# Places of moving operands modulo 256 bytes, and the order of two column widths, in a TensorE-bound decoder layer

## The chip, the core and the metric

The kernel runs on one core of one Trainium2 chip, in one launch. The metric is the device time of that launch in microseconds; the median of the runs shown is compared. The work is spread over the core's engines as the profile names them: PE (TensorE matmuls) with PEld (its weight loads), DVE (VectorE), ACT (ScalarE), POOL (GpSimd), and SP (SyncE, which here issues the DMAs).

## The reference

One layer of a decoder is computed for 1,024 prompt tokens and 64 sample tokens that share all weights:

```python
h = rmsnorm(x, norm_mix)
q, k, v, gu, gv, ga, gb = split_in(h @ w_in)
o = windowed attention of q, k, v          # window 128, per-head sinks
s = spatial_gating(gelu(gu), layernorm(gelu(gv)), ws, bs)
merged = sigmoid(ga) * (o @ w_pa) + sigmoid(gb) * (s @ w_pb)
x = x + merged @ w_out
z = rmsnorm(x, norm_ffn) @ w_up            # 5632 columns
c = conv_b + sum(zp[:, j:j + T] * conv_w[j] for j in range(3))
a, b = split(c)
x = x + (gelu(a) * b) @ w_down
y = rmsnorm(x, norm_final)
```

The model is 1,024 wide and the inner width of the feed-forward part is 2,816. Keys, values, the convolution's tails and the normalised gating values are further outputs.

## The kernel before

All data is float32. Every large product is made of three TensorE passes on split operands: an operand is split into a high part (written by ACT as type float32r) and a low part (the rest, by DVE), and high·high, high·low and low·high are added up in PSUM. The helper `split` at line 39 makes both parts; the names end in `h` and `l`. In each pass a 128×128 weight tile is loaded (LDWEIGHTS, one for every matmul) and a moving tile of 256, 288, 320 or 512 columns streams through.

The 1,088 tokens are worked in two groups: group 0 has 576 tokens (the 64 samples and 512 prompt tokens), group 1 has 512. The large projections use one level of a Strassen-like scheme of seven products on half-sized blocks. Its moving operands, called T, are sums of token blocks: for each of four inner blocks `kk` there are seven planes, of 288 columns for group 0 and of 256 columns for group 1, each in a high and a low version. The work runs through these stages:

1. The gating and value columns for all tokens (line 519, moving tiles of 256 columns).
2. The other columns of `w_in` by the seven products (`Chain.product`, matmul at line 301). A chain is one product's 12 matmuls: four `kk` times the three passes, all on one PSUM bank. For most weight pairs the chain of group 0 (12 matmuls of 288 columns) is followed by that of group 1 (12 of 256) on the same weights: 13 pairs × 7 products in this stage. For three weight pairs each group goes alone.
3. The gating branch and attention (lines 1168 to 1219), with the branch projection `branch` between, then two projections in `merge` and the output projection. Their matmuls stand in `mm3` at line 238: chunks of 320 and 256 columns for group 0, of 512 columns for group 1. The attention's product with the values at line 1219 has moving tiles of 512 columns as well.
4. The up projection, again `Chain.product` at line 301: 19 weight pairs with both chains, and three for which each group goes alone.
5. The down projection, also by seven products (`mm_dn`, matmul at line 1671). For each inner block `x` and each of four output blocks `m`, three matmuls of 288 columns (`e` = 0) stand before three of 256 (`e` = 1), from one T tile of 544 columns. The last four inner blocks of the last product are worked one width after the other.

So line 301 runs 32 × 7 = 224 products with a chain of 288 and a chain of 256 columns behind it, 42 chains of 288 columns alone and 42 of 256 alone.

What the change touches is where tiles lie in SBUF. A tile pool hands out addresses one after the other; `line(pool, n)` at line 246 takes n bytes of each partition that nobody uses, so that what is allocated next starts n bytes further. A weight tile starts in both programs at byte 32 modulo 256 (the addresses here and below are those that the two built programs carry). A T plane of group 0 has 288 × 4 = 1,152 bytes, which is 128 modulo 256; one of group 1 has 1,024 bytes, 0 modulo 256. In the kernel before the high T planes of one `kk` are one tile of seven planes and the low ones another, so that from plane to plane a group-0 operand lies 128 bytes further, modulo 256. Those are `t0_job` (line 653) for stage 2 and `t0_split` (line 1418) for stage 4.

Of the kernel before, what the change touches and what calls it, by code (L numbers as in the profile page):

```python
# [7 lines left out]
F32R = mybir.dt.float32r  # L8
# [7 lines left out]
P = 128  # L16
# [18 lines left out]
def layer(tc, a):  # L35
# [13 lines left out]
    with ExitStack() as top:  # L49
# [204 lines left out]

        def right(stack, name, bufs=1):
            return stack.enter_context(tc.tile_pool(name=name, bufs=bufs, side="right", reuse_waits="tile"))

        def combine(t4, b11, b12, b21, b22, eng=G):

# [107 lines left out]
        with ExitStack() as ph1:  # L367
# [285 lines left out]
            def t0_job(kk):  # L653
                def go():
                    first, t4, rest = sums_of(0, kk)
                    txa[0][kk] = th, tl = tuple(t0h.tile([P, 7, 288], F32R, name=f"t{y}{kk}") for y in "hl")
                    split(th[:, 0], tl[:, 0], first)
                    split(th[:, 1:5], tl[:, 1:5], t4)
                    split(th[:, 5:7], tl[:, 5:7], rest)
                    if kk == 3:  # L660
                        line(t0h, 32)
                return go

            def t1_job(kk):
# [322 lines left out]
            kvp["p"] = kvo.enter_context(tc.tile_pool(name="kv", bufs=1, reuse_waits="tile"))  # L987
            prep = prepare(groups[0])
            m1 = mo[1].enter_context(tc.tile_pool(name="mlp1", bufs=1, reuse_waits="tile"))
            line(m1, 64)  # L990
            b_order = [(0, 0), (1, 0), (0, 1), (1, 1)] + [(c, g) for c in range(2, KD) for g in range(2)]
            sgs, bst = {}, {}

# [55 lines left out]
            def attention(gr, pieces):  # L1049
# [102 lines left out]
                with tc.tile_pool(name=f"at{g}", bufs=1) as ap:  # L1152
                    steps = [(kv, i) for kv in range(NKV) for i in range(nblk)]
                    st = {}

                    def sc_p(kv, i):
                        if i == 0 and not has_s:
                            oh[kv], ol[kv] = (act.tile([P, 2, n], F32R, name=f"o{x}{kv}") for x in "hl")
                        b = gr["blk0"] + i
                        cur = P * i + (P if g else 0)  # L1160
                        k0 = cur - P if b else cur
                        o0 = 0 if b else P
                        ps = psm.tile([P, 1024], F32, name="sc")
                        ps = ps.rearrange("p (h j) -> p h j", h=4)
                        for h in range(4):
                            q = qt[2 * kv + h // 2][:, h % 2, P * i:P * i + P]
                            for e in range(2):
                                PE.matmul(ps[:, h, o0:256], q, kst[kv][:, e, k0:cur + P],  # L1168
                                          start=e == 0, stop=e == 1)
                        if i == 0 and kv:  # L1170
                            operands(gr, kv + 1)()
                        s = ap.tile([P, 4, P + 1], F32, name="s", bufs=3)
                        G.tensor_copy(s[:, :, P], late["sinkb"][:, 4 * kv:4 * kv + 4])
                        S.copy(s[:, :, 0:P], ps[:, :, P:256])
                        if b:
                            V.copy_predicated(s[:, :, 0:P], late["mprev"].to_broadcast([P, 4, P]),
                                              ps[:, :, 0:P])
                        else:
                            G.affine_select(s[:, :, 0:P], s[:, :, 0:P], [[0, 4], [-1, P]], ALU.is_ge, NEG,
                                            base=0, channel_multiplier=1)  # L1180
                        nm = ap.tile([P, 4], F32, name="nm", bufs=3)
                        V.tensor_reduce(nm, s, AX.X, ALU.max, negate=True)
                        dn = ap.tile([P, 4], F32, name="dn", bufs=3)
                        for h in range(4):
                            S.activation(s[:, h], s[:, h], AF.Exp, bias=nm[:, h:h + 1],  # L1185
                                         accum_out=dn[:, h:h + 1])
                        V.reciprocal(dn, dn)
                        V.tensor_mul(s[:, :, 0:P], s[:, :, 0:P], dn[:, :, None].to_broadcast([P, 4, P]))
                        st[kv, i] = s

                    def tr_p(kv, i):
                        s = st.pop((kv, i))
                        pt = psp.tile([P, 512], F32, name="pt")
                        for h in range(4):
                            PE.transpose(pt[:, h * P:h * P + P], s[:, h, 0:P], ident)  # L1195
                        ph = ap.tile([P, 512], F32R, name="ph")
                        pl = ap.tile([P, 512], F32R, name="pl")
                        split(ph, pl, pt)
                        b = gr["blk0"] + i
                        prev = vst[b - 1 if b else 0]  # L1200
                        parts = [(prev, ph), (prev, pl)]
                        if b:
                            for src, nm in ((ph, "h"), (pl, "l")):
                                t = ap.tile([P, 512], F32R, name=f"c{nm}")
                                G.affine_select(t.rearrange("p (h q) -> p h q", h=4),
                                                src.bitcast(F32).rearrange("p (h q) -> p h q", h=4),
                                                [[0, 4], [1, P]], ALU.is_ge, 0.0, base=0,
                                                channel_multiplier=-1)
                                parts.append((dvst[b], t))
                        st[kv, i] = parts  # L1210

                    def pv_p(kv, i, last):
                        if not last:
                            po = psp.tile([P, 512], F32, name="po")
                            st[kv, i] = po, st[kv, i]
                        po, parts = st[kv, i]
                        for e in (len(parts) - 1,) if last else range(len(parts) - 1):
                            v, t = parts[e]
                            PE.matmul(po, v[:, kv, :], t, start=e == 0, stop=last)  # L1219
                        if not last:  # L1220
                            return
                        st.pop((kv, i))
                        t = ap.tile([64, 512], F32, name="ot")
                        S.copy(t, po[64:128])
                        of = ap.tile([P, 2, P], F32, name="of", bufs=2)
                        tv = t.rearrange("p (a r q) -> p a r q", a=2, r=2)
                        pv = po[0:64].rearrange("p (a r q) -> p a r q", a=2, r=2)
                        for par in range(2):
                            V.tensor_add(of[64 * par:64 * par + 64], pv[:, :, par], tv[:, :, par])
                        c0 = soff + P * i  # L1230
                        split(oh[kv][:, :, c0:c0 + P], ol[kv][:, :, c0:c0 + P], of)

                    for i in range(len(steps) + 2):
                        if i >= 2:
                            tr_p(*steps[i - 2])
                        if i >= 3:
                            pv_p(*steps[i - 3], True)
                        fill()
                        if i < len(steps):
                            sc_p(*steps[i])  # L1240
                        fill()
                        if i >= 2:
                            pv_p(*steps[i - 2], False)
                    pv_p(*steps[-1], True)
# [26 lines left out]
            hmo = [ExitStack(), ExitStack()]  # L1271
            hmp = [hmo[g].enter_context(tc.tile_pool(name=f"hm{g}", bufs=1, reuse_waits="tile")) for g in (1, 0)][::-1]
            for pool in hmp:
                line(pool, 128)
            ms = [[], []]

            def operand(g):
# [140 lines left out]
            def t0_split(kk):  # L1418

                def go():  # L1420
                    x0, x1, t4 = hx.pop(kk)
                    tx[0][kk] = th, tl = tuple(t0p.tile([P, 7, 288], F32R, name=f"t{y}0{kk}") for y in "hl")
                    if kk % 2:
                        line(t0p, 96)
                    split(th[:, 0], tl[:, 0], x0[:, 0:288])
                    split(th[:, 5:7], tl[:, 5:7], x1.rearrange("p (h c) -> p h c", h=2))
                    split(th[:, 1:5], tl[:, 1:5], t4)
# [221 lines left out]
        with ExitStack() as ph3:  # L1649
# [9 lines left out]
                    nc.sync.dma_start(x[:, m], x1d[4 * dh + m][:, HT * th:HT * th + HT])  # L1659

            spans = ((0, 288), (288, HT))

            def place(m, e):
                b = bank[m] if e == 0 else bank[4 + m // 2]
# [109 lines left out]
            for at, j in enumerate(DN_ORDER):  # L1774
# [4 lines left out]
                for lo, hi in blocks:  # L1779
# [14 lines left out]
                    for mp in range(2) if hi - lo == 2 else (0,):  # L1794
                        for x in range(lo, hi):
                            for m in range(2 * mp, 2 * mp + 2) if hi - lo == 2 else range(4):
                                for e in range(2):
                                    mm_dn(m, e, x, got[x - lo], new)
                        if hi == NU:
                            for m in (2 * mp, 2 * mp + 1):  # L1800
# [109 lines left out]
```

## Time and profile before

| | before |
|---|---|
| runs, us | 1522.74, 1518.06, 1524.00 |
| median, us | 1522.74 |
| profiled execution: first to last instruction, us | 1519.4 |
| PE busy, us (share, matmuls) | 1503.9 (99%, 11,528) |
| PEld busy, us (share) | 1461.9 (96%) |
| DVE busy, us (share) | 1175.9 (77%) |
| ACT busy, us (share) | 850.5 (56%) |
| POOL busy, us (share) | 266.6 (18%) |

The profiled execution's own time is its span, 1519.4 us from the first to the last instruction; that is 3.3 us under the median of the runs and inside their spread. Times in the trace count from the span's start. An entry of a group of instructions names the line, the engine, the operation, the tiles (out, then in), the shapes and the count, then the busy time in us and the mean length of one in ns. The lengths of matmuls overlap, since they are pipelined: 0.28 to 0.30 us is shown for one that is followed by the next after 0.11 to 0.14 us. What a matmul costs is therefore read from the start of one row to the start of another, divided by the number of matmuls between them.

### The profile page before, as it was taken

Reading aid. Unit: us, or ns where it says so; the run is one execution under the profiler, and the core shown is the slowest. Engines: PE = TensorE matmul, PEld = TensorE weight load, DVE = VectorE, ACT = ScalarE, POOL = GpSimd, SP = SyncE. Lnnn points to the kernel's source line nnn. Section 1 sums busy time; section 2 is a strip of 40 time slices with the busy share of each in tenths; the row PEclk is TensorE's granted clock in tenths of the full one; section 3 lists DMA queues with packets and bytes.
Section 4 is the critical chain, followed back from the end, with each engine's and each line's share of the span. In section 5 each row is a group of like instructions: output and inputs, shape, how many; then the busy total and the mean of one; then the engine's idle time right before and its main releaser. Section 6 shows DMA issues by size and latency. Waiting matters only on the chain.

```text
span 1519.4 us, 30105 instructions
## 1 busy us (share of the span) xinstructions
PE 1503.9 (99%) x11528; PEld 1461.9 (96%) x11528; DVE 1175.9 (77%) x1897; ACT 850.5 (56%) x1767; POOL 266.6 (18%) x382
## 2 busy tenths in 40 slices
PE   9999999999999999999999999999999999999997
PEld 9999999999998989988989999999999999999997
DVE  7798877655576877979568988898898888785686
ACT  7557676654465675764344555655555556453452
POOL 0001000010030222210134322332132222000002
PEclk9999999999999999999999999999999999999999
DMA  7687446864779757449988333332232216973463
GB/s 253 210 280 272 154 164 222 243 212 142 245 245 290 223 162 250 153 138 308 330 281 278 129 117 116 124 116 100 108 128 104 108 58 234 367 251 97 117 182 122
DMA packets 135232, 289.88 MB, mean 191 GB/s; under 512 B 15537, under 2 KB 36849, under 8 KB 135089
## 3 DMA queue, kind: packets, MB, share of 16 engines
q1 hardware_dynamic: 134944, 287.96, 57.0%
q8 instruction: 90, 1.47, 0.4%
q14 instruction: 54, 0.43, 0.1%
q10 hardware_dynamic: 144, 0.01, 0.0%
HBM read 198.97 MB, written 90.92 MB: 191 GB/s over the span
## 4 chain that ended last, share of the span: by engine, by line
PE 84%; DVE 4%; DMA 4%; ACT 3%; issue 3%; POOL 1%; SPq 0%; POOLq 0%; ACTq 0%; DVEq 0%
PE st L301 44%; PE mm L238 15%; PE dn L1671 13%; PE st L519 6%; PE po L1219 2%; PE sc L1168 1%; DVE wl L41 1%; DMA v<-gvd 1%; PE pt L1195 1%; DMA wl<-upd 1%; POOL x L1734 1%; PE mx L803 1%; DMA vnd<-v 1%; ACT wh L41 1%; ACT s L1185 1%
## 5 line engine op out<-in xcount | busy, mean ns | idle before, releaser
L301 PE MATMUL st<-th,wh 128*128 128x288 f32 (+1 forms) x2128 | 611.6, 287 | 3.1 <-ACT kn L282 2.1
L301 PE MATMUL st<-tl,wh 128*128 128x288 f32 (+1 forms) x2128 | 609.4, 286 | 0.0
L301 PE MATMUL st<-th,wl 128*128 128x288 f32 (+1 forms) x2128 | 609.1, 286 | 0.3 <-DMA wl<-upd 0.3
L301 PEld LDWEIGHTS st<-th,wh 128*128 128x128 f32 x2128 | 400.3, 188 | 5.1 <-ACT kn L282 2.5
L301 PEld LDWEIGHTS st<-th,wl 128*128 128x128 f32 x2128 | 399.9, 188 | 0.5 <-DMA wl<-upd 0.5
L301 PEld LDWEIGHTS st<-tl,wh 128*128 128x128 f32 x2128 | 400.0, 188 | 0.0
L1671 PE MATMUL dn<-th,wh 128*128 128x288 f32 (+1 forms) x616 | 177.5, 288 | 1.0 <-ACT zb L327 0.7
L1671 PE MATMUL dn<-tl,wh 128*128 128x288 f32 (+1 forms) x616 | 176.8, 287 | 0.0
L41 ACT CAST wh<-wraw 128x512 fp32r<-128x512 f32 (+2 forms) x188 | 129.4, 701 | 83.6 <-PE mm L238 29.7
L1671 PE MATMUL dn<-th,wl 128*128 128x288 f32 (+1 forms) x616 | 174.6, 283 | 0.2 <-DVE wl L41 0.2
L41 DVE TENSOR_TENSOR wl<-wraw,wh 128x512 fp32r<-128x512 f32 (+2 forms) x188 | 148.6, 803 | 27.0 <-ACT wh L41 24.5
L41 DVE TENSOR_TENSOR wl<-ws,wh 128x512 fp32r<-128x512 f32 x168 | 117.9, 712 | 48.3 <-ACT wh L41 47.5
L41 ACT CAST wh<-ws 128x512 fp32r<-128x512 f32 x168 | 102.6, 621 | 92.6 <-PE st L301 59.6
L1671 PEld LDWEIGHTS dn<-th,wh 128*128 128x128 f32 x616 | 115.4, 187 | 1.5 <-ACT zb L327 0.9
L1671 PEld LDWEIGHTS dn<-th,wl 128*128 128x128 f32 x616 | 115.7, 188 | 0.4 <-DVE wl L41 0.4
L1671 PEld LDWEIGHTS dn<-tl,wh 128*128 128x128 f32 x616 | 115.7, 188 | 0.0
L519 PE MATMUL st<-w2h,hh 128*128 128x256 f32 x288 | 80.6, 282 | 0.6 <-ACT rst L485 0.4
L41 ACT CAST th<-traw 128x544 fp32r<-128x544 f32 (+1 forms) x85 | 54.5, 642 | 47.3 <-PE dn L1671 32.9
L519 PE MATMUL st<-w2l,hh 128*128 128x256 f32 x288 | 80.4, 280 | 0.0
L519 PE MATMUL st<-w2h,hl 128*128 128x256 f32 x288 | 79.8, 280 | 0.2 <-DVE hl L47 0.2
L41 DVE TENSOR_TENSOR tl<-traw,th 128x544 fp32r<-128x544 f32 (+1 forms) x85 | 61.1, 721 | 21.8 <-ACT th L41 21.2
L287 POOL TENSOR_TENSOR z<-kn,k 128x288 f32<-128x288 f32 (+1 forms) x32 | 30.1, 942 | 243.0 <-ACT kn L282 218.0
(271 smaller groups left out, 2935.2 us busy)
## 6 DMA issues: line engine op xcount, KB each, us to landing
wraw<-wt SPq DMA_DIRECT2D x137, 512.0 KB
traw<-td SPq DMA_DIRECT2D x77, 272.0 KB
td<-za SPq DMA_DIRECT2D x22, 544.0 KB
q<-qd SPq DMA_DIRECT2D x16, 512.0 KB
upd<-hl SPq DMA_DIRECT2D x14, 512.0 KB
td<-t SPq DMA_DIRECT2D x11, 544.0 KB
wpart<-wt SPq DMA_DIRECT2D x22, 256.0 KB
qd<-q SPq DMA_DIRECT2D x8, 576.0 KB
```

Of the source, the lines that this page charges most:

```text
L41: for x in (S.copy(hi, src), V.tensor_sub(lo, src, hi.bitcast(F32))):
L238: PE.matmul(ps[:, lo:lo + c1 - c0], u[:, k, :], v[:, c0:c1], start=(k == 0 and i == 0), stop=(k == nk - 1 and i == 2))
L287: op(to, pick(x, to, lo, hi), pick(y, to, lo, hi))
L301: PE.matmul(ps, u[:, kk, :], v, start=first and kk + i == 0, stop=kk == 3 and i == 2, skip_group_check=True)
L519: PE.matmul(ps, u[:, lo:lo + P], v[:, k, :], start=k + i == 0, stop=k == KD - 1 and i == 2)
L803: PE.matmul(ps[:, P * i:P * i + P], vn[:, i], late["wst"][:, c, :], start=True, stop=True)
L1168: PE.matmul(ps[:, h, o0:256], q, kst[kv][:, e, k0:cur + P], start=e == 0, stop=e == 1)
L1185: S.activation(s[:, h], s[:, h], AF.Exp, bias=nm[:, h:h + 1], accum_out=dn[:, h:h + 1])
L1195: PE.transpose(pt[:, h * P:h * P + P], s[:, h, 0:P], ident)
L1219: PE.matmul(po, v[:, kv, :], t, start=e == 0, stop=last)
L1671: PE.matmul(place(m, e), u[:, m, :], v[:, lo:hi], start=new and i + k == 0 and (e == 0 or m % 2 == 0), stop=i == NU - 1 and k == 2, skip_g ...
L1734: G.tensor_mul(xc, xc, rs)
```

## The change

Three things are altered.

- The T planes of group 0 go into one tile per `kk` of seven pairs of planes, high and low by turns (`both_planes`), in stage 2 and in stage 4. A pair has 2 × 1,152 bytes, 0 modulo 256, so every high plane has the same place, and every low plane lies 128 bytes further.
- Gaps are taken out, put in or made smaller, so that tiles that follow start elsewhere.
- In the down projection the two widths of one `m` are issued in one order for one `m` and in the other for the next (0 1, 1 0, 0 1, ...), by a flag `turn` that is flipped for every `m`.

```diff
+        def both_planes(pool, name):
+            t = pool.tile([P, 7, 2, 288], F32R, name=name)
+            return t[:, :, 0], t[:, :, 1]
...
-                    txa[0][kk] = th, tl = tuple(t0h.tile([P, 7, 288], F32R, name=f"t{y}{kk}") for y in "hl")
+                    txa[0][kk] = th, tl = both_planes(t0h, f"t{kk}")
...
-                    if kk == 3:
-                        line(t0h, 32)
...
-            line(m1, 64)
...
+                            if kv == NKV - 1:
+                                line(act, 192)
...
-                line(pool, 128)
+                line(pool, 64)
...
-                    tx[0][kk] = th, tl = tuple(t0p.tile([P, 7, 288], F32R, name=f"t{y}0{kk}") for y in "hl")
-                    if kk % 2:
-                        line(t0p, 96)
+                    tx[0][kk] = th, tl = both_planes(t0p, f"t0{kk}")
...
+            turn = [0]
...
-                                for e in range(2):
+                                turn[0] ^= 1
+                                for e in (1 - turn[0], turn[0]):
                                     mm_dn(m, e, x, got[x - lo], new)
```

Where the matmuls' moving tiles start, in bytes modulo 256 (weights at 32 unless noted):

| matmuls | columns | count | before | after |
|---|---|---|---|---|
| line 301, stage 2, group 0 | 288 | 1,344 | high 192 and low 64, or high 64 and low 192, by plane | high 224, low 96 |
| line 301, stage 4, group 0 | 288 | 1,848 | `kk` 0 and 1: high 32, low 160, or the reverse; `kk` 2 and 3: high 128, low 0, or the reverse | high 224, low 96 |
| line 301, group 1 | 256 | 3,192 | 224 | 224 |
| line 238, branch and output projection, group 1 | 512 | 336 | 96 | 32 |
| line 238, attention projection, group 1 | 512 | 192 | 224 | 32 |
| line 238, output projection, group 0 | 320 and 256 | 192 each | 224 | 96 |
| line 238, other two, group 0 | 320 and 256 | 336 each | 224 | 224 |
| line 1219, attention of group 0 | 512 | 56 | 128 | 64 |
| line 1219, attention of group 1 | 512 | 64 | 64, weights at 224 | 64 |
| line 1671, down projection | 288 and 256 | 924 each | 96 and 224 | 96 and 224 |

Apart from the two widths in the down projection, the additions that take its sums out of PSUM, and two neighbouring DMA issues there that change places, every engine gets the same instructions in the same order; the DVE and ACT instructions that write T planes of group 0 write runs of 288 columns with a stride instead of one long run.

## The prediction

> **What bounds the kernel now.** I read the page first, then who waits for whom on PE, then the groups with their shapes kept apart, and last the timeline of PE alone, row by row.
>
> ```profile
> span 1519.4 us, 30105 instructions
> PE 1503.9 (99%) x11528; PEld 1461.9 (96%) x11528; DVE 1175.9 (77%) x1897; ACT 850.5 (56%) x1767; POOL 266.6 (18%) x382
> PE   9999999999999999999999999999999999999997
> PEclk9999999999999999999999999999999999999999
> PE 84%; DVE 4%; DMA 4%; ACT 3%; issue 3%; POOL 1%; SPq 0%; POOLq 0%; ACTq 0%; DVEq 0%
> ```
>
> PE is busy in every slice at the full granted clock. It is the bound from end to end, and the chain that ended last runs 84% through it. The waits confirm that nobody keeps it:
>
> ```profile
> PE st L301 <- ACT kn L282: 2.1, 1, 2.1
> PE st L574 <- DVE c_ones L69: 1.2, 1, 1.2
> PE st L301 <- ACT k L280: 0.8, 3, 0.3
> ```
>
> The longest are 2.1, 1.2 and 0.8 us in total; nothing that feeds PE is worth more. So only the pace of the matmuls counts. Where it is spent:
>
> ```profile
> L301 PE MATMUL st<-th,wl 128*128 128x288 f32 x1064 | 314.9, 296 | 0.3 <-DMA wl<-upd 0.3
> L301 PE MATMUL st<-th,wh 128*128 128x256 f32 x1064 | 297.0, 279 | 0.9 <-ACT k L280 0.8
> L1671 PE MATMUL dn<-tl,wh 128*128 128x288 f32 x308 | 91.4, 297 | 0.0
> ```
>
> Each is one of three like groups (two with `th`, one with `tl`), so line 301 has 3 × 1,064 = 3,192 matmuls of 288 columns and as many of 256, and line 1671 has 924 of each width. 296 ns is a length that overlaps its neighbours; the pace is start to start. Four products from the two stages of line 301, one for each set of places that the 288-column tiles have now:
>
> ```profile
> 234.92 0.30 PE L301 MATMUL st<-th,wh 128*128 128x288 f32 x1
> ...
> 236.51 0.29 PE L301 MATMUL st<-th,wh 128*128 128x256 f32 x1
> ...
> 237.90 0.30 PE L301 MATMUL st<-th,wh 128*128 128x288 f32 x1
> ...
> 240.87 0.29 PE L301 MATMUL st<-th,wh 128*128 128x288 f32 x1
> ...
> 242.47 0.28 PE L301 MATMUL st<-th,wh 128*128 128x256 f32 x1
> ...
> 243.83 0.29 PE L301 MATMUL st<-th,wh 128*128 128x288 f32 x1
> ...
> 1031.16 0.29 PE L301 MATMUL st<-th,wh 128*128 128x288 f32 x1
> ...
> 1032.75 0.28 PE L301 MATMUL st<-th,wh 128*128 128x256 f32 x1
> ...
> 1034.14 0.29 PE L301 MATMUL st<-th,wh 128*128 128x288 f32 x1
> ...
> 1037.12 0.30 PE L301 MATMUL st<-th,wh 128*128 128x288 f32 x1
> ...
> 1038.72 0.28 PE L301 MATMUL st<-th,wh 128*128 128x256 f32 x1
> ...
> 1040.08 0.30 PE L301 MATMUL st<-th,wh 128*128 128x288 f32 x1
> ```
>
> Each set of three gives the chain of twelve 288s and the chain of twelve 256s behind it. In order, with the place of the last 288 modulo 256 in brackets: 1.59 + 1.39 (192), 1.60 + 1.36 (64), 1.59 + 1.39 (128), 1.60 + 1.36 (0). The 256s themselves lie at 224 every time. Two things are seen. A place changes the pace of the same instructions, at one clock and with no wait: the chain of 256s costs 1.36 or 1.39 by what streamed before it. And the sum hardly moves: 2.98, 2.96, 2.98, 2.96 us, mean 2.97.
>
> How far could it move? A stretch where 256s follow 256s only:
>
> ```profile
> 451.91 0.28 PE L301 MATMUL st<-th,wh 128*128 128x256 f32 x1
> ...
> 452.59 0.28 PE L301 MATMUL st<-th,wh 128*128 128x256 f32 x1
> ```
>
> Six in 0.68 us are 113.3 ns each, so 1.36 for twelve: the chain of 256s is then at the best pace shown. By columns that pace would be 113.3 × 288 / 256 = 127.5 ns for a 288, 1.53 for twelve. The 288s take 1.59 to 1.60, some 5 ns each above it. That excess is the prize.
>
> **The change part by part.** *T planes of group 0* (2,688 of them in the 224 products with both chains, 504 in the 42 chains alone). High goes to 224, low to 96. No row has 288s there at line 301. The nearest set is 192 and 64, the first above: 1.59 for the chain, against a mean of 1.595 over the four. The bounds are 1.53 from below (every excess gone) and 1.60 from above (the dearest of the four). I take 1.59. The last 288 of a chain then lies at 224, just where the 256s lie, as in the stretch of 256s alone; I take 1.36 for their chain, against a mean of 1.375, with 1.39 as the dearer row. Sum 2.95, that is 0.02 less per product, and 224 × 0.02 = 4.5 us saved. For the 42 lone chains I take nothing (42 × 0.005 = 0.2).
>
> The writes of T as strided runs, by ACT and DVE, cost PE nothing while those engines stand at 56% and 77%; the longest wait for ACT at line 301 is 2.1 us, the price if the cover were gone there once more.
>
> *Tiles of 512 columns at line 238.* 336 of them go from 96 to 32, and 192 from 224 to 32, where the weights start.
>
> ```profile
> 779.99 0.39 PE L238 MATMUL mm<-mh,wh 128*128 128x512 f32 x1
> ...
> 780.68 0.39 PE L238 MATMUL mm<-mh,wh 128*128 128x512 f32 x1
> ...
> 690.00 0.39 PE L238 MATMUL mm<-oh,wh 128*128 128x512 f32 x1
> 690.24 0.39 PE L238 MATMUL mm<-ol,wh 128*128 128x512 f32 x1
> 690.47 0.39 PE L238 MATMUL mm<-oh,wl 128*128 128x512 f32 x1
> ```
>
> At 96 three take 0.69, so 230 ns each; at 224 two take 0.47, 235. At 32 nothing is shown. From below: 2 × 113.3 = 226.7 each, so 336 × 3.3 + 192 × 8.3 = 2.7 us saved. From above: as much dearer than 235 as 230 is cheaper, 240, so 336 × 10 + 192 × 5 = 4.3 us lost. I take the cheaper row, 230, for all, as the tiles of 96 are nearer: 192 × 5 ns = 1.0 us saved. The 120 at line 1219 move too; at 5 ns either way that is 0.6 us, taken as nothing.
>
> *Pairs of 320 and 256 at line 238*, 192 of them, from 224 to 96:
>
> ```profile
> 729.95 0.42 PE L238 MATMUL mm<-mh,wh 128*128 128x320 f32 x2
> 730.21 0.43 PE L238 MATMUL mm<-ml,wh 128*128 128x320 f32 x2
> 730.48 0.31 PE L238 MATMUL mm<-mh,wl 128*128 128x320 f32 x1
> ```
>
> Two pairs take 0.53, 265 ns each; the best pace by columns would be 255. So 1.9 us from below, the same the other way as a bound above; I take nothing.
>
> *Down widths by turns.* Same matmuls and places, half as many changes of width.
>
> ```profile
> 1299.96 0.29 PE L1671 MATMUL dn<-th,wh 128*128 128x288 f32 x1
> ...
> 1300.36 0.28 PE L1671 MATMUL dn<-th,wh 128*128 128x256 f32 x1
> ...
> 1300.70 0.29 PE L1671 MATMUL dn<-th,wh 128*128 128x288 f32 x1
> ```
>
> Three 288s take 0.40, three 256s 0.34, which is 113 each: the 256s lose nothing at a change of width, and the 288s at 133 take what they take in long chains. So halving the changes should give nothing. From below, 288s at 127.5 would save 308 × 0.02 = 6 us; from above, 256s that lose 0.03 per run, as the dear chains above do, on half of 308 runs: 4.6 us. I take nothing. The additions that empty PSUM change order only; no wait of PE for them is among the rows.
>
> Sum: 4.5 + 0.2 + 1.0 = 5.7 us off 1519.4, so 1513.7. The median of the runs lies 3.3 us above the profiled span; the forecast for a median is 1517.0, or 0.4% faster.
>
> One rule speaks against all of it. The Trainium skill, page "TensorE: Matmul & The Clock Gate", section "Step-by-step: what each phase is for", says that TensorE has two independent read ports on SBUF, so that loading the next weights takes no read bandwidth from the running matmul. By that rule a moving tile's place relative to the weights is indifferent and the sum would be 0, the first rival below. The trace only half agrees: 1.36 against 1.39 for equal chains says that places do matter, though not that the weights' place does.
>
> **The rivals.** *Nothing* (about 1522): the sum of a product stays at 2.97, wherever the tiles lie. For it: four sets of places give 2.96 to 2.98, and what one chain saves the other loses. Against it: nothing in the rows forces the trade.
>
> *The excess goes* (about 1500): planes by turns at these places let the 288s run at 127.5 ns. 224 × (2.97 − 2.89) = 17.9, 42 × 0.06 = 2.5, and 2.7 at line 238 make 23 us. For it: 256s at 224 already run at that pace, and high planes and 256s now share their place. Against it: none of the four sets shown brings a 288 chain under 1.59. If a third to a half of it comes, the time is 1511 to 1515.
>
> [...]
>
> *The 256s lock in a dear pace* (about 1532). The last stretch of the down projection shows them so, at the same places:
>
> ```profile
> 1503.72 0.28 PE L1671 MATMUL dn<-tl,wh 128*128 128x256 f32 x1
> ...
> 1504.90 0.28 PE L1671 MATMUL dn<-th,wl 128*128 128x256 f32 x1
> ```
>
> Ten take 1.18, 118 ns each, without recovering. If the step from a 288 at 224 into the 256s leads there, their chain costs 1.42 instead of 1.375: 224 × 0.045 = 10 us lost, from which the time is slower than before as soon as the 288s save less than 45 ns per product. For it: nobody has yet entered the 256s from 224 with 288s. Against it: the four entries shown lose 0.03 at most and recover within the chain.
>
> **How the numbers follow.** About 0.5%, 7.6 us, is what a measurement of this kernel can tell from no change. Forecast, 0.45: 1517, own range 1511 to 1522; a third of it lies beyond 0.5%. Nothing, 0.15: within. The excess goes, 0.24: beyond. The dear pace, 0.16: beyond on the other side, but for 0.02. Faster 0.15 + 0.24 = 0.39, same 0.30 + 0.15 + 0.02 = 0.47, slower 0.14. The range reaches to most of both rivals, 1502 to 1529.
>
> **What would show it.** Right: the 256 chain behind 288s at 1.36 in every product, the 288 chain at 1.58 to 1.59, so products of 2.95; 512s at 230 or less; down blocks unchanged at 0.74; PE still at 99% with no new wait. Wrong: 288 chains of 1.56 or less (the excess goes), 256 chains over 1.40 (the dear pace), products of 2.97 (nothing), or a wait of PE for T tiles in the first products of either stage.

## The result, and the profile after

| | before | after |
|---|---|---|
| median of the runs taken side by side, us (22 each) | 1522.79 | 1518.63 |
| lowest and highest, us | 1518.06 to 1530.12 | 1516.38 to 1522.05 |
| ratio after / before, 95% interval | | 0.9977 (0.9967 to 0.9987) |
| profiled execution: span, us | 1519.4 | 1515.5 |

The kernel became 0.23% faster, 3.5 us by the ratio: less than the 0.5% that was named as the bound for telling a change from none. The interval does not reach 1, so some gain is there. The page of the changed kernel, its span, its first part, the granted clock and the chain that ended last:

```profile
span 1515.5 us, 30104 instructions
PE 1500.0 (99%) x11528; PEld 1459.7 (96%) x11528; DVE 1177.5 (78%) x1897; ACT 848.7 (56%) x1767; POOL 265.5 (18%) x382
PEclk9999999999999999999999999999999999999999
PE 83%; DVE 6%; ACT 4%; DMA 3%; issue 2%; POOL 1%; SPq 0%; POOLq 0%; ACTq 0%; DVEq 0%
```

The picture is that of before: PE is busy for 99% at the full clock. Who waited for whom on PE (total us, times, longest):

```profile
PE pt L1112 <- DVE s L1105: 1.5, 1, 1.5
PE st L578 <- DVE c_ones L69: 1.2, 1, 1.2
PE st L305 <- ACT k L284: 0.9, 3, 0.4
```

Nothing among them waits for T tiles, so the strided writes cost PE nothing and only the pace counts again. (Old line 301 is 305 now, old 519 is 523, old 1671 is 1673.) A product of the up projection, from PE's timeline; high and low planes are one tile `t` now, so two matmuls in a row on the same weights stand in one row, marked x2:

```profile
914.40 0.42 PE L305 MATMUL st<-t,wh 128*128 128x288 f32 x2
...
915.98 0.28 PE L305 MATMUL st<-th,wh 128*128 128x256 f32 x1
...
917.37 0.42 PE L305 MATMUL st<-t,wh 128*128 128x288 f32 x2
```

The chain of 288s takes 1.58, that of 256s 1.39, together 2.97: the old mean of 2.97, by another division. It is the same in nearly every product (mean 1.580 + 1.392). Tiles of 512 columns at line 238, in the attention projection and then in the output projection:

```profile
684.92 0.39 PE L238 MATMUL mm<-oh,wh 128*128 128x512 f32 x1
...
685.60 0.39 PE L238 MATMUL mm<-oh,wh 128*128 128x512 f32 x1
...
778.81 0.39 PE L238 MATMUL mm<-mh,wh 128*128 128x512 f32 x1
...
779.49 0.39 PE L238 MATMUL mm<-mh,wh 128*128 128x512 f32 x1
```

Three take 0.68 in both, 226.7 each, where the rows of before gave 235 and 230. And the down projection:

```profile
1362.14 0.29 PE L1673 MATMUL dn<-th,wh 128*128 128x288 f32 x1
...
1362.94 0.28 PE L1673 MATMUL dn<-th,wh 128*128 128x256 f32 x1
...
1363.62 0.29 PE L1673 MATMUL dn<-th,wh 128*128 128x288 f32 x1
```

Six 288s take 0.80 and six 256s 0.68, 0.74 for three and three as before. To see less than 10 ns per row I averaged the start-to-start times over whole stages of both traces:

| matmuls | before, ns | after, ns | change, us |
|---|---|---|---|
| line 301, 3,192 of 288 columns | 132.66 | 131.94 | −2.3 |
| line 301, 3,192 of 256 columns | 114.76 | 115.61 | +2.7 |
| line 238, attention projection, 192 of 512 | 233.3 | 226.8 | −1.25 |
| line 238, output projection, 192 of 512 | 229.5 | 227.4 | −0.4 |
| line 238, branch, 144 of 512 | 232.3 | 232.1 | 0 |
| line 1671, 924 of 256 | 114.46 | 113.68 | −0.7 |
| line 1671, 924 of 288 | 132.29 | 132.21 | −0.1 |
| line 519, 864 of 256 (not touched by the change) | | | −1.85, of it 1.0 in steps over 150 ns |

These add up to 3.9 us, the difference of the two spans. Long single steps are left out of the averages; over the rest of the kernel they cancel, the largest being +1.3 us in the branch and −1.3 us at line 301. And 1.85 of the 3.9 us lies in the first stage, which the change does not touch. In a second execution of the kernel before (`before_again`, below) the same stage was 1.87 us shorter than in the first, so this is a difference between executions. The view that shows it counts the stage's matmuls in the first 116 us (columns: stretch, its us, PE busy and matmuls, PEld busy and loads, granted clock, DMA share, GB/s). First the kernel before, then its second execution, then the changed kernel:

```profile
0.00:116.00 116.00, 102.87 (x864) 101.17 (x864) 1.00 0.76 249
```

```profile
0.00:116.00 116.00, 101.48 (x864) 100.26 (x864) 1.00 0.78 253
```

```profile
0.00:116.00 116.00, 101.34 (x864) 99.63 (x864) 1.00 0.78 254
```

Part of it is pace: of the 864 steps, 326 took 116 to 121 ns in the first of these, 162 in the second and 167 in the third, and nearly all others 113 or 114. The change itself shows 2.0 to 2.1 us, at the lower edge of the interval of the ratio (0.13% to 0.33%, 2.0 to 5.0 us).

### The profile page after: what moved, and what is told of

Read it like the earlier page. It is cut to its first block, busy times and chain, and to the rows that moved or that the text cites. A ratio compares the mean times of both kernels' runs of the same rounds, so it can differ in the third digit from the quotient of the medians.

```text
span 1515.5 us, 30104 instructions
## 1 busy us (share of the span) xinstructions
PE 1500.0 (99%) x11528; PEld 1459.7 (96%) x11528; DVE 1177.5 (78%) x1897; ACT 848.7 (56%) x1767; POOL 265.5 (18%) x382
## 4 chain that ended last, share of the span: by engine, by line
PE 83%; DVE 6%; ACT 4%; DMA 3%; issue 2%; POOL 1%; SPq 0%; POOLq 0%; ACTq 0%; DVEq 0%
PE st L305 45%; PE dn L1673 13%; PE mm L238 13%; PE st L523 6%; PE po L1222 2%; PE sc L1171 1%; DVE wl L41 1%; PE pt L1198 1%; DMA v<-gvd 1%; ACT wh L41 1%; PE mx L805 1%; DMA vnd<-v 1%; ACT s L1188 1%; DMA kd<-q 0%; DVE tl L41 0%
## 5 line engine op out<-in xcount | busy, mean ns | idle before, releaser
L305 PE MATMUL st<-t,wh 128*128 128x288 f32 x2128 | 429.8, 294 | 0.8 <-ACT kn L286 0.8
L305 PEld LDWEIGHTS st<-t,wh 128*128 128x128 f32 x2128 | 337.3, 188 | 1.9 <-ACT kn L286 1.0
L305 PE MATMUL st<-t,wl 128*128 128x288 f32 x1064 | 314.2, 295 | 0.0
L305 PE MATMUL st<-th,wh 128*128 128x256 f32 x1064 | 297.9, 280 | 1.0 <-ACT k L284 0.9
L305 PE MATMUL st<-tl,wh 128*128 128x256 f32 x1064 | 296.3, 278 | 0.0
L305 PE MATMUL st<-th,wl 128*128 128x256 f32 x1064 | 295.1, 277 | 0.0
L305 PEld LDWEIGHTS st<-th,wh 128*128 128x128 f32 x1064 | 200.7, 189 | 2.3 <-ACT k L284 1.8
L305 PEld LDWEIGHTS st<-th,wl 128*128 128x128 f32 x1064 | 200.7, 189 | 0.0
L305 PEld LDWEIGHTS st<-t,wl 128*128 128x128 f32 x1064 | 200.2, 188 | 0.0
L305 PEld LDWEIGHTS st<-tl,wh 128*128 128x128 f32 x1064 | 199.8, 188 | 0.0
```

The lines of the kernel that those rows point to most:

```text
L305: PE.matmul(ps, u[:, kk, :], v, start=first and kk + i == 0, stop=kk == 3 and i == 2, skip_group_check=True)
```

## The experiments

Three questions were open: which of the three edits carries the gain; whether it is the place itself or the distance to the weights that sets a pace; and whether a better set of places exists. Places are modulo 256 in bytes, weights at 32 unless noted; "past the weights" is the distance from them.

**One edit at a time.** First the T planes alone, on the kernel before (`planes`):

```diff
+            t = pool.tile([P, 7, 2, 288], F32R, name=name)
+            return t[:, :, 0], t[:, :, 1]
...
-                    txa[0][kk] = th, tl = tuple(t0h.tile([P, 7, 288], F32R, name=f"t{y}{kk}") for y in "hl")
+                    txa[0][kk] = th, tl = both_planes(t0h, f"t{kk}")
...
-                    tx[0][kk] = th, tl = tuple(t0p.tile([P, 7, 288], F32R, name=f"t{y}0{kk}") for y in "hl")
-                    if kk % 2:
-                        line(t0p, 96)
+                    tx[0][kk] = th, tl = both_planes(t0p, f"t0{kk}")
```

> The kernel before with only the T planes of group 0 by turns (high at 224, low at 96); 512-column tiles and down order as before. Theory (a trade inside each product): the 288 chain falls to 1.58 us, the 256 chain behind it rises to 1.39, the product stays at 2.97, and the time is that of before within 1 us (ratio 0.9993 to 1.0007). Rival (the planes carry the gain): ratio 0.998 or less.

Measured: median 1522.17 (11 runs) against 1521.93 of before (29), ratio 1.0009 (1.0000 to 1.0017). Its products have the division seen above, from its timeline:

```profile
914.32 0.42 PE L305 MATMUL st<-t,wh 128*128 128x288 f32 x2
...
915.90 0.28 PE L305 MATMUL st<-th,wh 128*128 128x256 f32 x1
...
917.29 0.42 PE L305 MATMUL st<-t,wh 128*128 128x288 f32 x2
```

1.58 + 1.39 = 2.97, and the interval leaves out the rival's 0.998: the planes carry no gain. One thing was not expected. Its down projection, same code and same places as before, ran slower in the profiled execution:

```profile
1321.42 0.30 PE L1671 MATMUL dn<-th,wh 128*128 128x288 f32 x1
...
1321.83 0.28 PE L1671 MATMUL dn<-th,wh 128*128 128x256 f32 x1
...
1322.18 0.30 PE L1671 MATMUL dn<-th,wh 128*128 128x288 f32 x1
```

0.41 + 0.35 = 0.76 instead of 0.74. From 1290 to 1440 us, 256s take 117.5 and 288s 133.6 on average, against 114.3 and 132.3; toward its end the stage gets quicker. From its first matmul to its last it takes 237.2 us against 233.7 before: 3.5 us more, as much as the whole effect under study.

Then the new places of the 512-column tiles alone, on the kernel before (`c512`):

```diff
-            line(m1, 64)
...
+                            if kv == NKV - 1:
+                                line(act, 192)
...
-                line(pool, 128)
+                line(pool, 64)
```

> The kernel before with only the new places of the tiles at lines 238 and 1219 (512 columns at 32, 192 pairs of 320 and 256 at 96). Theory (these places are worth their own pace): the attention projection's 512s run at 226.8 ns instead of 233.3 and the output projection's at 227.4 instead of 229.5, the branch's stay at 232; 1.7 us off, ratio 0.9989. Rival (the gain of the whole change comes from here): 3.5 us off, ratio 0.9977.

Measured: median 1519.38 (12 runs), ratio 0.9984 (0.9971 to 0.9998). The attention projection's 512s, from its timeline:

```profile
685.23 0.39 PE L238 MATMUL mm<-oh,wh 128*128 128x512 f32 x1
...
685.91 0.39 PE L238 MATMUL mm<-oh,wh 128*128 128x512 f32 x1
```

Three in 0.68, 226.7 each: by its paces this edit brings its 1.7 us by itself. The interval of the ratio holds both expectations, 0.9989 and 0.9977, and does not tell them apart. Its profiled execution had the slower down projection too (117.5 and 133.6).

The order of widths alone, on the kernel before (`turn`):

```diff
-                                for e in range(2):
+                                turn[0] ^= 1
+                                for e in (1 - turn[0], turn[0]):
```

> The kernel before with only the down widths by turns. Theory (a run of six 256s loses less at its start than two runs of three): 256s of the down projection at 113.7 ns instead of 114.5, 288s at 132.2 as before, 0.8 us off, ratio 0.9995. Rival (nothing changes): 114.5 and 132.3, ratio 1.0000.

Measured: median 1519.77 (11 runs), ratio 0.9991 (0.9982 to 0.9999); averaged over the down projection, 256s at 113.7 and 288s at 132.2, as expected. That edit is worth 0.7 us by these paces. The three ratios multiply to 0.9984, inside the interval of the changed kernel's 0.9977.

**Is it the distance to the weights?** The changed kernel with the weights alone moved, 32 to 96; every moving tile keeps its place modulo 256 (`w96`):

```diff
+        wgap = top.enter_context(tc.tile_pool(name="wgap", bufs=1))
+        wgap.tile([P, 16], F32, name="wgap0")
         W = Weights(top.enter_context(tc.tile_pool(name="wp", bufs=2)), 4, 4)
+        wgap2 = top.enter_context(tc.tile_pool(name="wgap2", bufs=1))
+        wgap2.tile([P, 48], F32, name="wgap1")
```

> The changed kernel with the weights alone moved from byte 32 to byte 96 modulo 256; every moving tile keeps its place. Theory 1 (pace is set by a moving tile's place relative to the weights): the attention projection's 512s, now 192 past the weights as they were before the change, go from 226.8 back to about 233 ns, and the products at line 301 leave 1.58 + 1.39. Theory 2 (pace is set by the moving tiles' own places and what streamed before): 226.8 and 1.58 + 1.39 stay, ratio to before as that of the change, 0.998.

Measured: median 1533.58 (4 runs), ratio 1.0076 (1.0061 to 1.0090). Its timeline in the attention projection and in a product:

```profile
691.07 0.39 PE L238 MATMUL mm<-oh,wh 128*128 128x512 f32 x1
...
691.77 0.39 PE L238 MATMUL mm<-oh,wh 128*128 128x512 f32 x1
...
923.24 0.43 PE L309 MATMUL st<-t,wh 128*128 128x288 f32 x2
...
924.83 0.28 PE L309 MATMUL st<-th,wh 128*128 128x256 f32 x1
...
926.24 0.29 PE L309 MATMUL st<-t,wh 128*128 128x288 f32 x1
```

Three 512s take 0.70: 233.3 by the stage's average, exactly what they took before the change, when they also lay 192 past the weights. And the chain of 256s, now 128 past the weights, takes 1.41, with single matmuls at 118 to 119 everywhere. Averaged over their stages, the products at line 301 cost 10 us more than in the changed kernel (9.2 of it in the 256s), the 256s of the down projection 4.1, and the 512s 2.6: 16.7 of the 17.9 us between the spans (1533.4 against 1515.5). Sixty-four bytes of the weights' place alone do this, so a moving tile's place by itself does not explain its pace. That it is the distance is shown best by the 512s: 233.3 at 192 past the weights by two different pairs of places. For the 256s there is one such pair: in the first stage they lie at 160 with their weights at 224, again 192 past, and take the same two paces, 113 to 114 and about 118, that they have at line 301 with 224 and 32. At the other distances each width was seen with one pair of places only.

**Does the slower down projection come with the execution?** The kernel before once more, unedited (`before_again`).

> The kernel before, looked at once more. Theory (its down projection runs at one of two paces, and which one differs from execution to execution): 256s at 114.3 and 288s at 132.3 ns, as in its first trace, or 117.5 and 133.6, as in the traces of planes and c512, whose down projection is the same; never between, and one pace over the whole stage. Rival (planes and c512 slow the down projection by themselves): 114.3 and 132.3 again.

Measured: one run, 1519.47, span 1517.8, with 256s at 114.3 and 288s at 132.3: the quicker pace. This does not tell the theories apart, since `planes` and `c512` were not profiled again. The view that shows the two paces at a glance counts the down projection's matmuls in the same 150 us of each trace (columns as in the first stage's view above). First the kernel before again, then `planes`, then the changed kernel:

```profile
1290.00:1440.00 150.00, 150.00 (x1218) 150.00 (x1217) 1.00 0.63 207
```

```profile
1290.00:1440.00 150.00, 150.00 (x1197) 150.00 (x1196) 1.00 0.63 208
```

```profile
1290.00:1440.00 150.00, 150.00 (x1223) 150.00 (x1223) 1.00 0.62 206
```

1,197 matmuls against 1,218 in the same time, at the same clock and the same DMA traffic: neither of those two makes the difference. Nor do the places: the down projection's matmuls have the same addresses in the kernel before, in `planes` and in `c512`. That it belongs to an execution rather than to a program is supported by the spread of `c512`: nine of its runs lie from 1516.7 to 1519.8 and three from 1522.9 to 1525.3, and the profiled one, with the slower pace, is one of the three. For the down projection it is not shown on one kernel with both paces profiled; for the first stage it is, by the 326 and 162 dear steps of the kernel before in its two executions.

**Other places for the planes.** On the changed kernel, a gap behind the last pair moves all planes of group 0 (`p96`, `p0` and `p64` by n = 128, 224 and 160; high planes then lie at 96, 0 and 64, low ones 128 further):

```diff
+                    if kk == 3:
+                        line(t0h, n)
...
+                    if kk == 3:
+                        line(t0p, n)
```

> The changed kernel with the T planes of group 0 moved by 128: high at 96, low at 224. Theory (the place of the last 288 decides what the 256s behind it lose; in the down projection 256s at 224 behind 288s at 96 lose next to nothing): the 256 chain at 1.36 to 1.37 us instead of 1.39, the 288 chain at 1.58 to 1.60, the product at 2.94 to 2.97. Rival (a product costs 2.97 wherever the planes lie): 2.97.

> The changed kernel with high planes at 0 and low at 128. Theory (place of the last 288): the 256 chain at 1.36, as behind a last 288 at 0 in the kernel before; the 288 chain at 1.58 to 1.60; product 2.94 to 2.96, up to 7 us off the changed kernel. Rival (a product costs 2.97 wherever the planes lie): the 288 chain rises to 1.61.

> The changed kernel with high planes at 64 and low at 192. Both are places that the kernel before has in its first stage, there for half of the products. Theory (place of the last 288 and of the chain): 1.594 + 1.37, product 2.96 to 2.97, 0 to 2 us off the changed kernel. Rival (a product costs 2.97 wherever the planes lie): 2.97.

Measured, one run each: 1524.13 (span 1522.4), 1516.83 (1515.1) and 1521.14 (1519.4). With high planes at 0 there are two kinds of product. Two of them from one execution of `p0`, an early one and a late one:

```profile
173.68 0.43 PE L305 MATMUL st<-t,wh 128*128 128x288 f32 x2
...
175.27 0.28 PE L305 MATMUL st<-th,wh 128*128 128x256 f32 x1
...
176.68 0.30 PE L305 MATMUL st<-t,wh 128*128 128x288 f32 x1
...
914.23 0.42 PE L305 MATMUL st<-t,wh 128*128 128x288 f32 x2
...
915.82 0.28 PE L305 MATMUL st<-th,wh 128*128 128x256 f32 x1
...
917.18 0.29 PE L305 MATMUL st<-t,wh 128*128 128x288 f32 x1
```

1.59 + 1.41 = 3.00 in the first, 1.59 + 1.36 = 2.95 in the second: the forecast's 2.95, though at another place than forecast, and the dear pace of the third rival, though at places that differ in nothing between the two. The dear kind comes in long stretches (about 55 chains early and 50 late of the 266). The quick products give back what those cost, so the span equals the changed kernel's. In `p64` the early products are dear as well (1.60 + 1.42) and the late ones quick (1.59 + 1.37); in `p96` about every other chain is, and a product takes 2.99 on average, so the expectation for it was missed. So was that for `p64` in its early stretch: 3.02, over both figures named. And `p64`, with widths by turns, has the slower down projection:

```profile
1364.31 0.30 PE L1677 MATMUL dn<-th,wh 128*128 128x288 f32 x1
...
1365.11 0.28 PE L1677 MATMUL dn<-th,wh 128*128 128x256 f32 x1
...
1365.81 0.30 PE L1677 MATMUL dn<-th,wh 128*128 128x288 f32 x1
```

Six 256s take 0.70 there, 117 each, against 0.68; in the last fifth of the stage they average about 115. So the order of widths does not by itself protect from the dear pace, and the pace can change inside one execution.

**Other places for group 1.** If 512s are quickest at the weights' place, so perhaps are the 256s, now at 224, 192 past them. The changed kernel with the T tiles of group 1 at 32 (`t32`, n = 64, last line removed) and at 96 (`t96`, n = 128, last line with 64):

```diff
+            line(t1h, n)
...
-        line(t1p, 192)
+        line(t1p, 64)
```

> The changed kernel with the T planes of group 1 (256 columns at line 301) moved from 224 to 32, the weights' place; group 0 stays at 224 and 96. Theory (a 256 has two steady paces, 113.3 and about 118, and the place relative to the weights says which can hold; 512s are cheapest at the weights' place): lone 256 chains at 1.36 throughout, product chains at 1.36 to 1.39, product 2.94 to 2.97. Rival (the weights' place is good for 512s alone): 256 chains at 1.41 to 1.42 as with the weights at 96, product 3.00, 7 us slower than the changed kernel.

> The changed kernel with the T planes of group 1 moved from 224 to 96, 64 past the weights and where a 288 at 224 ends. Theory (the step from the end of the last 288 to the start of the first 256 sets the loss on entering): no loss on entering, chain at 1.36, product 2.94. Rival (the place relative to the weights sets it): some other pace from the first chain on, 1.36 to 1.42, the same for lone chains as for those behind 288s.

Measured, one run each: 1532.60 (span 1530.9) and 1524.75 (1523.0); the kernel before, once beside them, took 1530.10, so the spans and paces are compared and not those times. A product of `t32`:

```profile
922.37 0.43 PE L305 MATMUL st<-t,wh 128*128 128x288 f32 x2
...
923.96 0.28 PE L305 MATMUL st<-th,wh 128*128 128x256 f32 x1
...
925.39 0.30 PE L305 MATMUL st<-t,wh 128*128 128x288 f32 x1
```

1.59 + 1.43 = 3.02. The 256s take 119.7 to 120.0 in every chain, also in those where no 288 has gone before: of the distances tried, the weights' place is the best for 512s and the worst for 256s, as the rival said. In `t96` they take 117.7 in all but three of some 260 chains, from the first on and in lone chains too, and products take 3.00: there too it is the rival that held. Both high planes at 0 and group 1 at 32 (`p0t32`, the edits of `p0` and `t32` together):

> High planes of group 0 at 0, low at 128, and the T planes of group 1 at 32. Theory (a 256 at the weights' place has one steady pace, 113.3): none of the long stretches at 118 that came with group 0 at 0 and group 1 at 224; product 2.95, 5 us off the changed kernel. Rival (two paces everywhere): stretches of chains at 1.41 between such at 1.36.

Measured: one run, 1535.06 (span 1533.3); 256s at 119 to 120, products 1.61 + 1.43 = 3.03, and the slower down projection (117.7). It missed the numbers of both theories.

**Without the planes.** Since the planes brought nothing, the last kernel is the changed one with the T planes laid out as before (`noplanes`: the edits of `c512` and `turn` together).

> The changed kernel with the T planes of group 0 put back as they were before; new places at lines 238 and 1219 and down widths by turns stay. Theory (the planes only trade 288s against 256s): products at 2.97 as before and after, 512s of the attention projection at 226.7 ns, down 256s at 113.3 where the stage is in its faster pace; 2.5 us off the kernel before, ratio 0.998, the changed kernel's own ratio of 0.9977 within the interval. Rival (the planes carry what the two other parts leave over): 0.999 or more.

Measured: median 1518.25 (8 runs) against 1522.83 (11), ratio 0.9978 (0.9964 to 0.9992), span 1516.4. 512s of its output projection:

```profile
779.33 0.39 PE L238 MATMUL mm<-mh,wh 128*128 128x512 f32 x1
...
780.01 0.39 PE L238 MATMUL mm<-mh,wh 128*128 128x512 f32 x1
```

226.7 each; its down projection has 113.7 and 132.2 on average. It does what the changed kernel does, with two edits of the three. No kernel of the twelve is clearly quicker than the changed one.

## Why the prediction was right or wrong

The time, 1518.63 against 1517.0, came out near the forecast, but not by its sum, and in that it was luck: the term that made up most of the sum gave nothing, and two smaller terms that were taken too low, with differences between executions, filled most of its place.

*What bounds the kernel.* Right. PE at 99%, full clock, no wait of note, in every profile; every difference found is one of pace.

*T planes of group 0, 4.5 of the 5.7 us.* This is the step that failed: "I take 1.36 for their chain", because the last 288 would lie at 224, like the 256s. It took 1.39, the dearer row that the step had named. On entering from a 288 at 224 a chain's first five steps are 118 to 123 ns, before it settles at 113; about 32 ns are lost per chain. The 288s were quicker than forecast (1.581 against 1.59), and the two cancel: +0.4 us by the averages, 1.0009 by the runs with this edit alone. The first rival, that a product stays at 2.97 wherever tiles lie, is thus what happened to the products. But the forecast's argument against it holds too: nothing forces the trade, since `p0` shows 1.59 + 1.36 in its quick stretches and `w96` or `t32` over 3.00. The 0.2 us for the lone chains is in the forecast's sum although its text takes nothing for them.

*512s, taken at 230 for all.* Right in sign, mis-sized: 226.7 to 227.4 in the two projections at the weights' place, near the lower bound, 1.7 us instead of 1.0. The branch's did not move (232, where 230 was taken). Of the rest at line 238, the pairs of 320 and 256 stayed as forecast.

*Down widths, taken as nothing.* "The 256s lose nothing at a change of width" came from 0.34 for three, which a row's 10 ns cannot resolve; averaged, they lost 1.2 ns each, and the change took 0.8 of that: 0.7 us. What was missed is that nearly the whole stage can run at the dear pace that the third rival had seen in its last stretch, which costs 3.5 us from one trace to the next, more than any edit here. Whether widths by turns make it rarer stays open: with them, with the weights at 32, seven traces had the quick pace and `p64` and `p0t32` the slow one; without them, both traces of the kernel before had the quick one, `planes` and `c512` the slow one.

*The rivals.* The excess of the 288s went nowhere: at every place tried their chains take between 131.8 and 133.9 ns per matmul, never 127.5. The dear pace is real, at 117.7 to 120 ns, but did not come to the products of the changed kernel: two of its 266 chains stayed in it. The argument against it was weaker than it read: in the kernel before some 15 of the 266 chains, outside the rows shown, were in it already and stayed in it to their end.

*The rule on read ports.* By the Trainium skill, page "TensorE: Matmul & The Clock Gate", section "Step-by-step: what each phase is for", loading weights takes no read bandwidth from the running matmul, since there are two independent ports. What the prediction drew from it, that the place relative to the weights is indifferent, does not hold here: with the weights alone moved by 64 bytes, 512s went from 226.7 to 233.3 ns, the kernel from 1518.6 to 1533.6 us. That the two reads take bandwidth from each other is not shown by this; only that the weights' place sets the pace.

*What stays open.* The changed kernel's interval reaches to 5.0 us, its own edits show 2.0 to 2.1 in the averages; the rest cannot be told from the differences between executions in the first stage and in the down projection. Why a distance favours one width and harms another was not found.

## What to carry to other kernels

When PE is busy all the time and nothing waits, compare start-to-start times over a whole stage for each place and each width, not lengths and not single rows: here 0.7 ns times 3,192 is already 2 us. Place moving tiles by their distance to the weights and measure each width by itself, and sum a chain with the chain behind it, for what one gained the other lost. Before crediting an edit with 0.2%, look whether a stage that it does not touch changed its pace between the two traces.

## What the runs showed of the hardware

Steady paces in ns by the distance past the weights modulo 256, float32r, one weight load per matmul, full clock (a dash where none was measured):

| columns | 0 | 64 | 128 | 192 |
|---|---|---|---|---|
| 256 | 120.0 (`t32`) | 117.7 (`t96`) | 118 to 119 (`w96`) | 113.3 or about 117.7 (before, `p0`) |
| 512 | 226.7 (after) | 225 to 232 by turns, 229.5 on average (before) | – | 233.3 (before, `w96`) |

The 512s here are those of the attention and output projections; the branch's averaged 232 at 0 and at 64. At 192 the 256s have two paces at the same places and clock: they enter the dear one in long stretches and leave it, in one and the same execution (`p0`, `p64`). In the down projection both paces were seen at the same DMA share too (0.63). Weight tiles shifted by 64 bytes cost the changed kernel about 1% (1.0076 against 0.9977, both to the kernel before).
